# Attention scores of a two-layer hybrid decoder: the keys' high and low parts in one moving operand, the halves summed by VectorE, and attention's stages at later steps

## The chip, the cores and the metric

The kernel runs on one core of a Trainium2 chip. The metric is device time in microseconds (us) of one execution; before the change the median of three runs is 844.93 us (844.09 to 846.22). One more execution was taken with the hardware profiler: it took 844.57 us, of which 842.7 us lie between its first and last instruction. All times inside the kernel are read from that execution.

## The reference

Two decoder layers on 256 tokens of width 2048. The first mixes tokens by forgetting attention (FoX: 32 heads of 64, logits with a decay term), the second by sliding-window attention (SWA: 32 query heads on 4 key heads, window 128, a sink per head, rotary on 16 of 64 dims). Cut to what matters:

```python
# layer 0, per head: causal, 256 keys
s = jnp.einsum('bqhd,bkhd->bhqk', qi.astype(jnp.float32), kf) * scale
s = s + ci[..., None] - c[:, :, None, :]
s = jnp.where(mask[None, None], s, NEG_INF)
p = jax.nn.softmax(s, axis=-1).astype(v.dtype)
return jnp.einsum('bhqk,bkhd->bqhd', p, v)

# layer 1, per head: the block's own 128 keys and the 128 before
m = jnp.maximum(jnp.max(s, axis=-1, keepdims=True), sink)
e = jnp.exp(s - m)
denom = jnp.sum(e, axis=-1, keepdims=True) + jnp.exp(sink - m)
p = (e / denom).astype(v.dtype)

# both layers
p = h @ w_in; ...; y = y * jax.nn.silu(gate); x = x + y @ w_out
```

Everything is float32, with RMSNorm before each layer and at the end.

## The kernel before, in words

**Matrix products in two parts.** Each float32 operand of a projection is split into a high part (a copy in the fp32r format) and a low part (the rest). Activations are split once (`xs`, `ys`: slot 0 high, slot 1 low); each loaded weight tile is split when it arrives: ScalarE casts the high part (L203), VectorE subtracts it (L204), into one of five `w` buffers. A projection is cut into units of 16 input tiles of 128 channels, in parts of four tiles. `block` (around L220) issues, for one part and one half `c` of the unit's columns, four matmuls with a moving operand of 512 columns (high and low side by side: the product of the high stationary part with both) and four with 256 columns (low stationary part, high moving part). The 512-column result has two halves, which the consumers add (`low_half`, L251).

**Order of the work.** TensorE follows the program order of `block` calls over one long stream: FoX input units (q, k, gate, v of eight groups of four heads), the output projection of layer 0, SWA units (k, v, then q and gate of eight groups), the output projection of layer 1. A step counter ticks after every second matmul of a block, so four times per block. Attention is hung on that counter: `after(steps, fn)` runs `fn` so many steps later, with high priority. A group's two pairs of heads (`Pair`, j = 0 and 1) have their score step `s` and transpose steps `t` and `t + 4` in tables: `FOX_DUE = ((16, 34), (40, 60), 106)` means pair 0 scores at 16 and transposes at 34 and 38, pair 1 at 40 and 60, and the values product at 106. `FOX_FIRST` and `FOX_LAST` hold for the first and last FoX group, `SWA_DUE` and `SWA_LAST` for layer 1. For VectorE and ScalarE a scheduler lays the instructions in a fixed order ahead of the run; each engine then takes its own row strictly in that order.

**A pair before the change.** `score` (matmuls at L74) computes, for two heads `hh` and two query blocks (128 queries on 128 keys, 128 queries on 256 keys), query (stationary, its 64 high and 64 low dims stacked) times the keys' high part, then their low part into the same accumulator: eight matmuls, four of 128 and four of 256 columns, in the two buffers of the PSUM pool `ps_s`. `biased` (L293) adds the bias or mask on VectorE and takes the row maximum, in one instruction per head and block. ScalarE exponentiates with row sums (`exps`, L303), VectorE divides (`normalise`: reciprocal L311, four multiplications L314), TensorE transposes the probabilities (`pt`, L77, six transposes of 128x128), ScalarE copies them out (`pts`, L357). `Group.values` multiplies them with v (`psy`), VectorE multiplies by the gate (L389), ScalarE and VectorE write both parts of `ys` (L390, L391).

Of the kernel before, what the change touches and what calls it, by code (L numbers as in the profile page):

```python
# [35 lines left out]
BIAS = 14  # L36
SCALE_DUE = 8


FOX_DUE = ((16, 34), (40, 60), 106)  # L40
FOX_FIRST = ((46, 70), (76, 96), 116)
FOX_LAST = ((14, 32), (38, 72), 86)
SWA_DUE = ((16, 40), (44, 64), 74)
SWA_LAST = ((26, 45), (30, 56), 68)
WBUFS = 5
LOOK = WBUFS - 2
NEG = -1e30
LOWEST = -3.4e38
SCALE = HD ** -0.5
# [3 lines left out]
def trunk(  # L53
# [16 lines left out]
    nc = tc.nc  # L70


    def mm(*args, **kw):
        tc.keep_in_program_order(nc.tensor.matmul(*args, **kw))  # L74
# [26 lines left out]
    def after(steps, fn):  # L101
        due.setdefault(clock[0] + max(steps, 1), []).append(fn)
# [82 lines left out]
    state = {}  # L185
# [23 lines left out]
    def block(unit, p, c):  # L209
# [14 lines left out]

        first, last = kt0 == 0, kt0 + s == KT
        ops = [operands(i) for i in range(s)]
        if unit.halves:

# [55 lines left out]

    BLK = ((slice(0, P), 0), (slice(P, 3 * P), 1))

    def biased(pss, bias, scale):

        st = work.tile([P, 2, 3 * P], F32, tag="st", name="st")
        mx = work.tile([P, 2, 2], F32, tag="mx", name="mx")  # L290
        for hh in range(2):
            for rng, qb in BLK:
                nc.vector.tensor_tensor_reduce(  # L293
                    out=st[:, hh, rng], in0=pss[hh][:, rng], in1=bias(hh, rng), scale=scale,
                    scalar=LOWEST, op0=ALU.add, op1=ALU.max, accum_out=mx[:, qb, hh : hh + 1],
                )
        return st, mx

    def exps(st, nm):
        l = work.tile([P, 2, 2], F32, tag="l", name="l")  # L300
        for hh in range(2):
            for rng, qb in BLK:
                nc.scalar.activation(  # L303
                    st[:, hh, rng], st[:, hh, rng], AF.Exp,
                    bias=nm[:, qb, hh : hh + 1], accum_out=l[:, qb, hh : hh + 1],
                )
        return l

    def normalise(st, l):
        rl = work.tile([P, 2, 2], F32, tag="rl", name="rl")  # L310
        nc.vector.reciprocal(rl, l)  # L311
        for hh in range(2):
            for rng, qb in BLK:
                nc.vector.tensor_scalar_mul(st[:, hh, rng], st[:, hh, rng], rl[:, qb, hh : hh + 1])  # L314

# [8 lines left out]
            nc.vector.tensor_sub(q2[other, hh, :], t[w, :], q2[w, hh, :].bitcast(F32))  # L324
        return q2

    def score(pss, q2, kk):

        for rng, qb in BLK:
            keys = rng.stop - rng.start  # L330
            for hh in range(2):
                q = q2[:, hh, qb * P : (qb + 1) * P]
                for part in range(2):
                    mm(
                        pss[hh][:, rng], q, kk[hh][:, part, 0:keys],
                        start=part == 0, stop=part == 1,
                    )

    class Pair:


        def __init__(self, j, scores, prepare=None):
            self.j, self.scores, self.prepare = j, scores, prepare

        def early(self):
            self.bias = self.prepare()

        def s(self):
            self.st = self.scores()

        def t(self, hh, group):
            pt = ps_t.tile([P, 512], F32, tag="T", name="pt")
# [4 lines left out]
            nc.scalar.copy(group.pts[hh][:, self.j, :], pt[:, 0 : 3 * P])  # L357

        def later(self, group, s, t):
            if self.prepare is not None:  # L360
                after(s - BIAS, self.early)
# [38 lines left out]
    ones_row, z, a = (once[0:H, i * S : (i + 1) * S] for i in range(3))  # L400
# [33 lines left out]
    class FoxGroup(Group):  # L434
# [13 lines left out]
        def k(self, c, ps):  # L448
# [32 lines left out]
        def pair(self, j):  # L481
            h0 = 4 * self.g + 2 * j

            def bias():

                assert "forgot" in state
                bc = fox.tile([P, 2, 3 * P], F32, tag="bc", name="bc")
                nc.gpsimd.dma_start(out=bc, in_=negc_d[h0 : h0 + 2, :].partition_broadcast(P))  # L488
                for hh in range(2):
                    diagonal = bc[:, hh, :].rearrange("p (b k) -> p b k", k=P)[:, 0:3:2, :]  # L490
                    filled = fill_where_not(diagonal, [[0, 2], [-1, P]], 0, 1)
                if h0 == SINK:
# [4 lines left out]
            def scores():  # L497
                pss = [ps_s.tile([P, 512], F32, tag="S", name="ps_s") for _ in range(2)]
                kk = self.kT[j]
                score(pss, self.qT[j], (kk[:, 0], kk[:, 1]))  # L500
                bc = made.bias
                st, mx = biased(pss, lambda hh, rng: bc[:, hh, rng], 1.0)

                c2 = cq[:, :, h0 : h0 + 2]
                nc.vector.tensor_add(mx, mx, c2)  # L505
                nc.vector.tensor_sub(mx, c2, mx)  # L506
                normalise(st, exps(st, mx))
                return st

            made = Pair(j, scores, bias)  # L510
            return made

        def v_of(self, j, b, hh):
            return self.vg[b][:, (2 * j + hh) * HD : (2 * j + hh + 1) * HD]
# [203 lines left out]
    class SwaGroup(Group):  # L718
# [6 lines left out]
        def q(self, c, ps):  # L725
# [3 lines left out]
            if c == 0:  # L729
                self.attend(2 * self.u, SWA_LAST if self.u == 7 else SWA_DUE, self.u == 7, True)  # L730

        def pair(self, j):
            h0 = 4 * self.u + 2 * j
            kv = self.u // 2

            def scores():
                pss = [ps_s.tile([P, 512], F32, tag="S", name="ps_s2") for _ in range(2)]
                kk = state["kk"][:, kv]
                score(pss, self.qT[j], (kk, kk))
                st, mx = biased(pss, lambda hh, rng: smask[:, rng], SCALE)  # L740
# [8 lines left out]
                normalise(st, l)  # L749
                return st  # L750

            return Pair(j, scores)

        def v_of(self, j, b, hh):
            kv = self.u // 2
# [56 lines left out]
    start = [(u, p) for p in range(2) for u in (v0, q0, k0)] + [(v0, 2), (v0, 3), (q0, 2), (k0, 2)]  # L812
# [26 lines left out]
    smask = cpool.tile([P, 3 * P], F32, name="smask")  # L839
# [86 lines left out]
```

## Time and profile before

| what | value |
|---|---|
| median of three runs | 844.93 us |
| profiled execution, its own time | 844.57 us |
| its span, first to last instruction | 842.7 us |
| TensorE (PE) busy | 830.5 us, 99% |
| VectorE (DVE) busy | 656.7 us, 78% |
| ScalarE (ACT) busy | 544.0 us, 65% |
| matmuls | 4970, of them 256 for scores |
| granted TensorE clock | 0.998 |

"Busy" is the share of the span in which an engine executes something. Matmuls overlap, so the time of a stretch of matmuls is best read from the start of the first to the start of what follows. PE is TensorE, PEld its weight loads, DVE VectorE, ACT ScalarE, POOL GpSimd, SP the queue that issues the weight transfers. An entry in square brackets behind a row of the timeline says how long the engine had been idle and what released it.

### The profile page before, as it was taken

Reading aid. Unit: us, or ns where it says so; the run is one execution under the profiler, and the core shown is the slowest. Engines: PE = TensorE matmul, PEld = TensorE weight load, DVE = VectorE, ACT = ScalarE, POOL = GpSimd, SP = SyncE. Lnnn points to the kernel's source line nnn. Section 1 sums busy time; section 2 is a strip of 40 time slices with the busy share of each in tenths; the row PEclk is TensorE's granted clock in tenths of the full one; section 3 lists DMA queues with packets and bytes.
Section 4 is the critical chain, followed back from the end, with each engine's and each line's share of the span. In section 5 each row is a group of like instructions: output and inputs, shape, how many; then the busy total and the mean of one; then the engine's idle time right before and its main releaser. Section 6 shows DMA issues by size and latency. Waiting matters only on the chain.

```text
span 842.7 us, 13482 instructions
## 1 busy us (share of the span) xinstructions
PE 830.5 (99%) x4970; PEld 720.8 (86%) x4970; DVE 656.7 (78%) x1380; ACT 544.0 (65%) x1067; POOL 67.3 (8%) x93
## 2 busy tenths in 40 slices
PE   9999999999999999999999999999999999999996
PEld 7888888888888888888888888888888888888885
DVE  5899868678686877867677778788898889876555
ACT  6678757667475765746655655567766776666552
POOL 1022101001010010100011110000000000003211
PEclk9999999999999999999999999999999999999999
DMA  8666555555464554554465554543444434355522
GB/s 279 239 229 244 188 180 173 190 186 196 157 225 162 171 213 161 187 191 145 162 214 192 200 184 165 180 170 133 167 150 151 157 143 167 133 186 177 194 100 101
DMA packets 26385, 150.51 MB, mean 179 GB/s; under 512 B 3232, under 2 KB 5440, under 8 KB 10704
## 3 DMA queue, kind: packets, MB, share of 16 engines
q1 hardware_dynamic: 23904, 142.22, 48.2%
q0 software_dynamic: 1408, 6.36, 2.2%
q10 hardware_dynamic: 1008, 1.07, 0.4%
q8 instruction: 39, 0.64, 0.3%
q14 instruction: 26, 0.21, 0.1%
HBM read 147.50 MB, written 2.15 MB: 178 GB/s over the span
## 4 chain that ended last, share of the span: by engine, by line
PE 92%; DVE 4%; DMA 1%; ACT 1%; issue 1%; SPq 1%; DVEq 0%; ACTq 0%
PE acc L74 83%; PE ps_s L74 3%; PE psy L74 3%; PE pt L77 2%; DVE w L204 1%; DMA wraw<-in_vf_dram 1%; DMA wraw<-in_fox_in_dram 1%; SPq L198 0%; DVE st L293 0%; ACT st L303 0%; ACT w L203 0%; DVE q L324 0%; DVE xs L155 0%; DVE scaled L669 0%; PE ps_n L74 0%
## 5 line engine op out<-in xcount | busy, mean ns | idle before, releaser
L74 PE MATMUL acc<-xs,w 128*128 128x256 f32 (+1 forms) x2624 | 484.1, 339 | 0.7 <-ACT w L203 0.7
L74 PEld LDWEIGHTS acc<-xs,w 128*128 128x128 f32 x2624 | 405.8, 189 | 61.0 <-issue 3.9
L204 DVE TENSOR_TENSOR w<-wraw,w 128x1024 fp32r<-128x1024 f32 (+4 forms) x275 | 325.7, 1188 | 107.6 <-ACT w L203 105.6
L203 ACT CAST w<-wraw 128x1024 fp32r<-128x1024 f32 (+4 forms) x275 | 278.3, 1016 | 135.6 <-PE acc L74 120.6
L74 PE MATMUL acc<-ys,w 128*128 128x512 f32 x960 | 170.8, 338 | 0.0
L74 PEld LDWEIGHTS acc<-ys,w 128*128 128x128 f32 x960 | 147.4, 189 | 21.5 <-issue 0.6
L74 PE MATMUL acc<-w,xs 128*128 128x256 f32 (+2 forms) x608 | 115.1, 335 | 0.9 <-DVE w L204 0.4
L74 PEld LDWEIGHTS acc<-w,xs 128*128 128x128 f32 x608 | 94.2, 189 | 12.7 <-ACT w L203 1.0
L251 ACT COPY half<-acc 128x256 f32<-128x256 f32 x112 | 41.3, 369 | 58.0 <-PE acc L74 57.3
L303 ACT ACTIVATE st<-st,mx 128x128 f32<-128x128 f32 (+1 forms) x128 | 56.7, 445 | 13.8 <-DVE mx L506 8.4
L575 POOL TENSOR_TENSOR acc<-acc,sq 128x256 f32<-128x256 f32 x28 | 29.8, 1065 | 105.3 <-ACT sq L569 105.3
L357 ACT COPY pts<-pt 128x384 f32<-128x384 f32 x64 | 30.4, 475 | 10.5 <-PE pt L77 10.3
L74 PE MATMUL ps_s<-kk,q 128*128 128x128 f32 (+1 forms) x256 | 35.8, 281 | 0.2
L314 DVE TENSOR_SCALAR st<-st,rl 128x128 f32<-128x128 f32 (+1 forms) x128 | 32.8, 319 | 1.1
L74 PEld LDWEIGHTS ps_s<-kk,q 128*128 128x128 f32 x256 | 32.1, 190 | 1.2 <-issue 0.4
L77 PE MATMUL pt<-ident,st 128*128 128x128 f32 x192 | 31.8, 273 | 1.1 <-DVE st L314 1.1
L573 POOL COPY acc<-sq 128x256 f32<-128x256 f32 x2 | 1.9, 934 | 334.0 <-ACT sq L569 334.0
L121 POOL TENSOR_SCALAR_AFFINE_SELECT bc<-bc 128x256 f32<-128x256 f32 x32 | 22.6, 725 | 51.8 <-DMA bc<-negc_d 51.8
L77 PEld LDWEIGHTS pt<-ident,st 128*128 128x128 f32 x192 | 23.1, 140 | 3.8 <-ACT st L303 1.5
L488 POOL DMA_DIRECT2D bc<-negc_d x16 | 8.8, 552 | 216.3 <-DVE mx L505 139.6
L323 ACT CAST q<-qT 64x256 fp32r<-64x256 f32 x32 | 12.8, 401 | 18.6 <-DVE qT L699 18.2
L155 DVE SCALAR_TENSOR_TENSOR xs<-xT,g_sb,xs 128x256 fp32r<-128x256 f32 x32 | 22.0, 710 | 3.0 <-ACT xs L154 3.0
(133 smaller groups left out, 577.9 us busy)
## 6 DMA issues: line engine op xcount, KB each, us to landing
wraw<-in_fox_in_dram SPq DMA_DIRECT2D x58, 1024.0 KB, 4.9
wraw<-in_swa_in_dram SPq DMA_DIRECT2D x36, 1024.0 KB, 4.8
wraw<-in_fox_out_dram SPq DMA_DIRECT2D x14, 1024.0 KB, 4.9
wraw<-in_swa_out_dram SPq DMA_DIRECT2D x14, 1024.0 KB, 4.9
bc<-negc_d POOLq DMA_DIRECT2D x16, 384.0 KB, 3.9
wraw<-in_fox_in_dram SPq DMA_DIRECT2D x4, 512.0 KB, 5.5
wraw<-in_fox_out_dram SPq DMA_DIRECT2D x4, 512.0 KB, 3.6
wraw<-in_swa_out_dram SPq DMA_DIRECT2D x4, 512.0 KB, 3.5
```

The lines of the kernel that those rows point to most:

```text
L74: tc.keep_in_program_order(nc.tensor.matmul(*args, **kw))
L77: tc.keep_in_program_order(nc.tensor.transpose(out, in_, ident))
L121: return nc.gpsimd.affine_select(out=ap, in_=ap, compare_op=ALU.is_ge, fill=NEG, base=base, pattern=pattern, channel_multiplier=mult,)
L155: nc.vector.scalar_tensor_tensor(out=xs[:, kt, 1, :], in0=xT[:, kt, :], scalar=g, in1=xs[:, kt, 0, :].bitcast(F32), op0=ALU.mult, op1=ALU. ...
L203: state["split"] = nc.scalar.copy(w[:, :, 0, :], raw)
L204: nc.vector.tensor_tensor(out=w[:, :, 1, :], in0=raw, in1=w[:, :, 0, :].bitcast(F32), op=ALU.subtract)
L251: nc.scalar.copy(s, ps[:, S : 2 * S])
L303: nc.scalar.activation(st[:, hh, rng], st[:, hh, rng], AF.Exp, bias=nm[:, qb, hh : hh + 1], accum_out=l[:, qb, hh : hh + 1],)
L314: nc.vector.tensor_scalar_mul(st[:, hh, rng], st[:, hh, rng], rl[:, qb, hh : hh + 1])
L323: nc.scalar.copy(q2[w, hh, :], t[w, :])
L357: nc.scalar.copy(group.pts[hh][:, self.j, :], pt[:, 0 : 3 * P])
L575: nc.gpsimd.tensor_add(sums[0], sums[0], s)
```

## The change

**Scores.** The keys' high and low parts become one moving operand: for the block of 256 keys one matmul per head with 512 columns, for the block of 128 keys one with 256 columns. The two halves of a result are then two products that have to be added. VectorE adds the low half and the bias into `st` (`tensor_add`, L354 and L365 of the changed kernel), and then reduces as before with `st` in the place of the bias (L340). A pair takes three `ps_s` buffers in turn where it took two, and it is done in two steps: the 256-key block at `s`, the 128-key block (`s_first`) `SECOND = 8` steps later, followed by the softmax.

**SWA's division** goes from VectorE to ScalarE: four `nc.scalar.mul` per pair with the reciprocal as a per-row scale (L306).

**Steps.** All five tables move score, transpose and value steps later by 0 to 28 steps.

```diff
-FOX_FIRST = ((46, 70), (76, 96), 116)
-SWA_LAST = ((26, 45), (30, 56), 68)
+FOX_FIRST = ((46, 76), (80, 108), 122)
+SWA_LAST = ((20, 50), (36, 66), 82)
+SECOND = 8
...
-                nc.vector.tensor_tensor_reduce(
-                    out=st[:, hh, rng], in0=pss[hh][:, rng], in1=bias(hh, rng), scale=scale,
-                    scalar=LOWEST, op0=ALU.add, op1=ALU.max, accum_out=mx[:, qb, hh : hh + 1],
-                )
...
+                if scalar:
+                    nc.scalar.mul(p, p, r)
+                else:
+                    nc.vector.tensor_scalar_mul(p, p, r)
...
-                for part in range(2):
-                    mm(
-                        pss[hh][:, rng], q, kk[hh][:, part, 0:keys],
-                        start=part == 0, stop=part == 1,
-                    )
...
+        def product(self, out, hh, qb, keys):
+            q2, kk = self.operands()
+            mm(out, q2[:, hh, qb * P : (qb + 1) * P], kk[hh][:, :, 0:keys], start=True, stop=True)
+        def reduce(self, high, hh, rng, qb):
+            st = self.st[:, hh, rng]
+            nc.vector.tensor_tensor_reduce(
+                out=st, in0=high, in1=st, scale=self.scale, scalar=LOWEST,
+                op0=ALU.add, op1=ALU.max, accum_out=self.mx[:, qb, hh : hh + 1],
+            )
         def s(self):
...
+            for hh in range(2):
+                self.product(pss[hh], hh, qb, S)
+            for hh in range(2):
+                nc.vector.tensor_add(self.st[:, hh, rng], pss[hh][:, S:], self.bias[:, hh, rng])
+                self.reduce(pss[hh][:, 0:S], hh, rng, qb)
+            after(SECOND, self.s_first)
+        def s_first(self):
...
+            for hh in range(2):
+                self.product(ps[:, hh], hh, qb, P)
+            nc.vector.tensor_add(self.st[:, :, rng], ps[:, :, 1, :], self.bias[:, :, rng])
+            for hh in range(2):
+                self.reduce(ps[:, hh, 0, :], hh, rng, qb)
+            self.soft(self.st, self.mx)
```

How the instructions stand, at three places. First TensorE at the first FoX pair's scores (`ps_s`), between blocks of a projection (`acc`); before:

```order
L74 MATMUL acc<-xs,w 128x512 x4
L74 MATMUL acc<-xs,w 128x256 x4
L74 MATMUL ps_s<-kk,q_505 128x128 x4
L74 MATMUL ps_s<-kk,q_505 128x256 x4
L74 MATMUL acc<-xs,w 128x512 x4
```

And in the changed kernel:

```order
L76 MATMUL acc<-xs,w 128x256 x4
L76 MATMUL ps_s<-kk,q_505 128x512 x2
L76 MATMUL acc<-xs,w 128x512 x4
L76 MATMUL acc<-xs,w 128x256 x4
L76 MATMUL acc<-xs,w 128x512 x4
L76 MATMUL acc<-xs,w 128x256 x4
L76 MATMUL ps_s<-kk,q_505 128x256 x2
L76 MATMUL acc<-xs,w 128x512 x4
```

Eight matmuls have become four, and the second two stand two blocks (eight steps) behind the first two.

Second VectorE in the same pair, from its last reduction to the reciprocal (`rl`); `mx` is the row maximum that ScalarE's exponentials wait for, `w` a weight split, `gt` and `gate_e` the gate; before:

```order
L293 ISA st,mx<-ps_s,bc 128x256
L293 ISA mx 128x1
L264 SCALAR_TENSOR_TENSOR gate_e<-gt,gate_e 128x512
L505 TENSOR_TENSOR mx<-mx,cq 128x4
L506 TENSOR_TENSOR mx<-cq,mx 128x4
L204 TENSOR_TENSOR w<-wraw,w 128x4x256
L311 RECIPROCAL rl<-l 128x4
L314 TENSOR_SCALAR st<-st,rl 128x128
```

In the changed kernel, from behind the second addition (`st<-ps_s,bc`, L365) to the reciprocal:

```order
L206 TENSOR_TENSOR w<-wraw,w 128x4x256
L340 ISA st,mx<-ps_s,st 128x128
L340 ISA mx 128x1
L340 ISA st,mx<-ps_s,st 128x128
L340 ISA mx 128x1
L270 TENSOR_TENSOR gt<-gt,gate_e 128x512
L518 TENSOR_TENSOR mx<-mx,cq 128x4
L206 TENSOR_TENSOR w<-wraw,w 128x4x256
L519 TENSOR_TENSOR mx<-cq,mx 128x4
L461 TENSOR_TENSOR q<-acc,half 128x256
L463 TENSOR_TENSOR q<-q,r_494 128x256
L301 RECIPROCAL rl<-l 128x4
```

Two weight splits and a gate multiplication now stand ahead of the second `mx` row, where one gate row stood.

Third TensorE at the last SWA group's values product (`psy`). The part `w_7901` before (`w_7891` after) is the first one that reads the channel tiles 14 and 15 of `ys`, which this product yields; before:

```order
L74 MATMUL psy_7921<-pts_7860,vs_5376 64x512
L74 MATMUL psy_7921<-pts_7860,vs_5376 64x2x128
L74 MATMUL acc_7904<-ys_81,w_7836 128x512 x4
L74 MATMUL acc_7904<-ys_81,w_7836 128x256 x4
L74 MATMUL acc_7945<-ys_81,w_7805 128x512 x4
L74 MATMUL acc_7945<-ys_81,w_7805 128x256 x4
L74 MATMUL acc_7904<-ys_81,w_7870 128x512 x4
L74 MATMUL acc_7904<-ys_81,w_7870 128x256 x4
L74 MATMUL acc_7945<-ys_81,w_7836 128x512 x4
L74 MATMUL acc_7945<-ys_81,w_7836 128x256 x4
L74 MATMUL acc_7808<-ys_81,w_7901 128x512 x4
```

And in the changed kernel:

```order
L76 MATMUL psy_7960<-pts_7875,vs_5376 64x512
L76 MATMUL psy_7960<-pts_7875,vs_5376 64x2x128
L76 MATMUL acc_7934<-ys_81,w_7836 128x256 x4
L76 MATMUL acc_7777<-ys_81,w_7891 128x512 x4
L76 MATMUL acc_7777<-ys_81,w_7891 128x256 x4
```

Four whole blocks stood between the values product and its first reader; now four matmuls of 256 columns do.

More of the change, by code (lines that the diff above doesn't have):

```diff
@@ L37 @@
 SCALE_DUE = 8
-FOX_DUE = ((16, 34), (40, 60), 106)
-FOX_FIRST = ((46, 70), (76, 96), 116)
-FOX_LAST = ((14, 32), (38, 72), 86)
-SWA_DUE = ((16, 40), (44, 64), 74)
-SWA_LAST = ((26, 45), (30, 56), 68)
+FOX_DUE = ((16, 44), (48, 74), 106)
+FOX_FIRST = ((46, 76), (80, 108), 122)
+FOX_LAST = ((14, 40), (44, 72), 88)
+SWA_DUE = ((20, 56), (52, 88), 102)
+SWA_LAST = ((20, 50), (36, 66), 82)
+SECOND = 8
 WBUFS = 5
@@ L285, in trunk @@
     BLK = ((slice(0, P), 0), (slice(P, 3 * P), 1))
[L287 to L293, printed above, removed]
-                    out=st[:, hh, rng], in0=pss[hh][:, rng], in1=bias(hh, rng), scale=scale,
-                    scalar=LOWEST, op0=ALU.add, op1=ALU.max, accum_out=mx[:, qb, hh : hh + 1],
-                )
-        return st, mx
     def exps(st, nm):
@@ L307, in exps, with normalise @@
         return l
-    def normalise(st, l):
+    def normalise(st, l, scalar):
         rl = work.tile([P, 2, 2], F32, tag="rl", name="rl")
@@ L313, in normalise @@
             for rng, qb in BLK:
-                nc.vector.tensor_scalar_mul(st[:, hh, rng], st[:, hh, rng], rl[:, qb, hh : hh + 1])
+                p, r = st[:, hh, rng], rl[:, qb, hh : hh + 1]
+                if scalar:
+                    nc.scalar.mul(p, p, r)
+                else:
+                    nc.vector.tensor_scalar_mul(p, p, r)
     TOP, BOTTOM = slice(0, HD), slice(HD, P)
@@ L325, in stack_q, with __init__ @@
         return q2
[L327 to L332, printed above, removed]
-                for part in range(2):
-                    mm(
-                        pss[hh][:, rng], q, kk[hh][:, part, 0:keys],
-                        start=part == 0, stop=part == 1,
-                    )
     class Pair:
-        def __init__(self, j, scores, prepare=None):
-            self.j, self.scores, self.prepare = j, scores, prepare
+        def __init__(self, j, operands, scale, soft, prepare):
+            self.j, self.operands, self.scale, self.soft = j, operands, scale, soft
+            self.prepare = prepare
@@ L345, in early @@
         def early(self):
             self.bias = self.prepare()
-        def s(self):
-            self.st = self.scores()
+        def product(self, out, hh, qb, keys):
[7 more added lines that the diff above has]
+            )
@@ new lines, in s @@
+        def s(self):
+            self.st = work.tile([P, 2, 3 * P], F32, tag="st", name="st")
+            self.mx = work.tile([P, 2, 2], F32, tag="mx", name="mx")
+            rng, qb = BLK[1]
+            pss = [ps_s.tile([P, 512], F32, tag="S", name="ps_s") for _ in range(2)]
+            for hh in range(2):
[4 more added lines that the diff above has]
+            after(SECOND, self.s_first)
@@ L351, in t @@
+        def s_first(self):
+            rng, qb = BLK[0]
+            ps = ps_s.tile([P, 512], F32, tag="S", name="ps_s")
+            ps = ps.rearrange("p (h a k) -> p h a k", h=2, k=P)
+            for hh in range(2):
[4 more added lines that the diff above has]
+            self.soft(self.st, self.mx)
         def t(self, hh, group):
@@ L359, in later @@
         def later(self, group, s, t):
-            if self.prepare is not None:
-                after(s - BIAS, self.early)
+            after(s - BIAS, self.early)
             after(s, self.s)
@@ L495, in bias, with soft @@
                 return bc
[L497 to L502, printed above, removed]
+            def soft(st, mx):
                 c2 = cq[:, :, h0 : h0 + 2]
@@ L506, in scores, with operands @@
                 nc.vector.tensor_sub(mx, c2, mx)
[L507 to L511, printed above, removed]
+                normalise(st, exps(st, mx), False)
+            def operands():
+                kk = self.kT[j]
+                return self.qT[j], (kk[:, 0], kk[:, 1])
+            return Pair(j, operands, 1.0, soft, bias)
         def v_of(self, j, b, hh):
@@ L734, in pair, with soft @@
             kv = self.u // 2
[L736 to L740, printed above, removed]
+            def soft(st, mx):
                 sk = sink[:, h0 : h0 + 2].unsqueeze(1).to_broadcast([P, 2, 2])
@@ L748, in scores, with operands @@
                 nc.vector.tensor_add(l, l, es)
-                normalise(st, l)
-                return st
-            return Pair(j, scores)
+                normalise(st, l, True)
+            def operands():
+                kk = state["kk"][:, kv]
+                return self.qT[j], (kk, kk)
+            mask = smask.unsqueeze(1).to_broadcast([P, 2, 3 * P])
+            return Pair(j, operands, SCALE, soft, lambda: mask)
         def v_of(self, j, b, hh):
```

## The prediction

> **What bounds the kernel now.** I read the page first: shares of the engines and the chain that ended last.
>
> ```profile
> span 842.7 us, 13482 instructions
> PE 830.5 (99%) x4970; PEld 720.8 (86%) x4970; DVE 656.7 (78%) x1380; ACT 544.0 (65%) x1067; POOL 67.3 (8%) x93
> ...
> PE 92%; DVE 4%; DMA 1%; ACT 1%; issue 1%; SPq 1%; DVEq 0%; ACTq 0%
> ```
>
> TensorE is busy from end to end and carries 92% of the chain. So time is won by giving TensorE less to do, and lost by making it wait. Next, what TensorE waits for, and its two largest waits with a releaser:
>
> ```profile
> PE rows L74 <- DVE tail L656: 2.5, 1, 2.5
> PE warm L74 <- DVE ones L114: 1.1, 1, 1.1
> PE pt L77 <- DVE st L314: 1.1, 1, 1.1
> ```
>
> After the start, attention costs it one visible wait: 1.1 us ahead of one set of transposes (`pt`), released by VectorE's division. Then the price of a matmul, from starts in the timeline and one long piece of the chain:
>
> ```profile
> 741.54 0.63 PE L74 MATMUL acc<-ys,w 128*128 128x512 f32 x2
> 742.01 0.49 PE L77 MATMUL pt<-ident,st 128*128 128x128 f32 x3
> ...
> 416.41 90.01 PE acc L74 x512
> ```
>
> Two 512-column matmuls take 742.01 - 741.54 = 0.47 us, 0.235 us each. The long piece has as many of 512 as of 256 columns and takes 90.01/512 = 0.176 us each, so a pair takes 0.352 and the 256-column one 0.117. A block of four and four: 1.41 us, for four steps. The scores of one pair of heads:
>
> ```profile
> L74 PE MATMUL ps_s<-kk,q 128*128 128x128 f32 (+1 forms) x256 | 35.8, 281 | 0.2
> ...
> 593.29 1.09 PE L74 MATMUL ps_s<-kk,q 128*128 128x128 f32 x8
> 594.22 8.58 PE L74 MATMUL acc<-xs,w 128*128 128x512 f32 x48
> ```
>
> Eight matmuls take 594.22 - 593.29 = 0.93 us. Four of 256 columns are 0.47 of it, so the four of 128 columns take 0.46, 0.115 each: as much as twice the columns.
>
> **The change part by part.** *TensorE.* Per pair, two matmuls of 512 columns (0.47) and two of 256 (0.23) replace the eight: 0.70 in place of 0.93. All of this is on the path. 256/8 = 32 pairs times 0.23 gives **-7.2 us**. Bounds: 0.21 to 0.25 per pair, 6.7 to 8.0.
>
> [...]
>
> *VectorE and ScalarE.* Nearest rows:
>
> ```profile
> L275 DVE TENSOR_TENSOR gt<-acc,half 128x256 f32<-128x256 f32 x32 | 13.4, 420 | 1.8 <-ACT half L251 1.7
> L293 DVE CUSTOM_DVE_ANT_0 st<-ps_s,bc 128x256 f32<-128x256 f32 x32 | 13.4, 419 | 0.0
> L293 DVE CUSTOM_DVE_ANT_0 st<-ps_s,bc 128x128 f32<-128x128 f32 x32 | 9.1, 286 | 1.0 <-PE ps_s L74 1.0
> ...
> 600.39 1.01 DVE L314 TENSOR_SCALAR st<-st,rl 128x128 f32<-128x128 f32 x4
> ...
> L617 ACT ACTIVATE xT<-xT,g_sb 128x256 f32<-128x256 f32 x14 | 7.1, 510 | 0.4
> L653 ACT ACTIVATE diag<-ident,tail 128x128 f32<-128x128 f32 x2 | 0.8, 402 | 0.1
> ```
>
> Three additions that read PSUM, 256 columns each, at 0.42 make 1.26 us of VectorE per pair. The reductions keep their shapes. SWA's division, 1.01 us of VectorE per pair, leaves for ScalarE, 2 x 0.51 + 2 x 0.40 = 1.82. Sums: VectorE +40.3 - 16.2 = +24 us, ScalarE +29 us. Off the path both, so the price is nothing where the stage has room. The stages (first FoX group, a middle FoX group, an SWA group; engines in the order PE, PEld, DVE, ACT, POOL):
>
> ```profile
> 58.00:109.00 51.00, 49.95 (x310) 43.32 (x309) 46.30 (x111) 38.58 (x85) 11.56 (x17) 1.00 0.63 215
> 208.40:258.10 49.70, 49.70 (x302) 43.37 (x301) 37.93 (x77) 31.95 (x62) 3.80 (x6) 1.00 0.53 186
> 589.60:616.80 27.20, 27.20 (x166) 23.19 (x164) 24.30 (x67) 19.16 (x43) 0.00 (x0) 1.00 0.44 153
> ```
>
> Middle FoX group: 37.93 + 2 x 1.26 = 40.5 of 49.2 us; room. SWA group: VectorE 24.30 + 2.52 - 2.02 = 24.8, ScalarE 22.8, of 26.7; little room. The first stage has four pairs in it: 46.30 + 5.0 = 51.3 us, where TensorE would need 51.0 - 4 x 0.23 - 1.05 = 49.0. VectorE is full there, so I expect TensorE to wait there. The first pair's rows show where:
>
> ```profile
> 59.44 1.08 PE L74 MATMUL ps_s<-kk,q 128*128 128x128 f32 x8
> ...
> 64.11 0.28 DVE L293 CUSTOM_DVE_ANT_0 st<-ps_s,bc 128x128 f32<-128x128 f32 x1
> ...
> 65.22 0.68 DVE L264 SCALAR_TENSOR_TENSOR gate_e<-gt,gate_e 128x512 f32<-128x512 f32 x1
> ...
> 66.01 0.16 DVE L506 TENSOR_TENSOR mx<-cq,mx 128x4 f32<-128x4 f32 x1
> 66.09 1.22 DVE L204 TENSOR_TENSOR w<-wraw,w 128x1024 fp32r<-128x1024 f32 x1
> 66.21 0.40 ACT L303 ACTIVATE st<-st,mx 128x128 f32<-128x128 f32 x1 [0.42 <-DVE mx L506]
> ...
> 68.11 0.18 DVE L311 RECIPROCAL rl<-l 128x4 f32<-128x4 f32 x1 [0.80 <-ACT st L303]
> 68.33 1.01 DVE L314 TENSOR_SCALAR st<-st,rl 128x128 f32<-128x128 f32 x4
> 68.78 0.59 PE L77 MATMUL pt<-ident,st 128*128 128x128 f32 x3
> ...
> 81.05 0.61 PE L77 MATMUL pt<-ident,st 128*128 128x128 f32 x3 [1.05 <-DVE st L314]
> ```
>
> VectorE reaches the first pair at 64.11, late, behind older work which the change leaves. In the new order it then does two additions and two reductions (1.68), the gate row (0.68), the third addition (0.42), a split (1.22), two short reductions (0.57), a gate row (0.68), `mx` (0.16), a split (1.22), `mx` (0.16): 6.8 us, up to 70.9. Exponentials up to the reciprocal take 68.11 - 66.21 = 1.90, then 0.22 and the first multiplication 0.29: 73.3. Starts lie closer than durations (1.11 us for four reductions of 1.41), so 72.7 to 73.3. TensorE arrives at the transposes 30 steps after 59.44: seven blocks and a half block of four 512-column matmuls plus the scores, 9.8 + 0.94 + 0.70, at 70.9. It waits about 2.0 us, where it waited for nothing. The second pair waited 1.05 before, with 20 steps behind its whole product; it now has 20 behind the second part of it, two splits in its chain too, but less old work ahead: 0.7 (0 to 1.5) in my estimate. The third gets nothing to 0.8. Together 2.7 for 1.05: **+1.6 us** (bounds -1 to +3.5). The windows' argument, 51.3 - 49.0 = 2.3 us of waiting, lies close to it.
>
> *Layer 1's second pair.* TensorE has, between its second product and its transposes (28 steps), seven blocks and the next group's first product, 7 x 1.41 + 0.47 = 10.3 us. Before:
>
> ```profile
> 605.62 7.16 PE L74 MATMUL acc<-xs,w 128*128 128x512 f32 x40
> ...
> 611.81 1.01 DVE L314 TENSOR_SCALAR st<-st,rl 128x128 f32<-128x128 f32 x4
> 612.61 0.49 PE L77 MATMUL pt<-ident,st 128*128 128x128 f32 x3
> ```
>
> From the end of the scores, 605.62, the first head was divided at about 612.4: 6.8 us. Now an addition and two short reductions replace four (-0.2), ScalarE's two multiplications for that head take 0.9 for 0.6 (+0.3), and two weight splits can stand in the chain (+2.4): 9.3 of 10.3 us. So no wait; the cover is 1 us. The longer cut through a pair also needs `ps_s` back eight steps after the first product, 2.8 us, and two additions and a reduction are 1.3 us: no wait unless VectorE comes 1.5 us late.
>
> *The tail.* The last group's second scores waited for their buffers; and its values product now stands closer to its reader:
>
> ```profile
> 735.53 1.49 PE L74 MATMUL ps_s<-kk,q 128*128 128x128 f32 x8
> 736.86 0.40 PE L74 MATMUL acc<-xs,w 128*128 128x256 f32 x2
> ...
> 752.80 3.54 PE L74 MATMUL acc<-ys,w 128*128 128x512 f32 x18
> ...
> 753.68 0.75 DVE L389 TENSOR_TENSOR gt<-psy,gt 128x256 f32<-128x256 f32 x2
> 754.13 0.74 ACT L390 CAST ys<-gt 128x256 fp32r<-128x256 f32 x2 [1.63 <-DVE gt L389]
> 754.57 0.76 DVE L391 TENSOR_TENSOR ys<-gt,ys 128x256 fp32r<-128x256 f32 x2
> ```
>
> The first wait, 736.86 - 735.53 - 0.93 = 0.40, goes, as the two pairs are now 16 steps apart. After the values product, `ys` for tile 14 is complete at 755.0, 2.2 us later. Before, four blocks covered it, 5.6 us. Now four 256-column matmuls and the two 512-column ones of tiles 12 and 13 do: 0.47 + 0.47 = 0.94. TensorE waits about 1.0 us (0.7, if VectorE is free at once, to 1.3). Net **+0.6**.
>
> **Sum**: -7.2 + 1.6 + 0.6 = -5.0. The profiled execution took 844.57 us, 0.36 below the median of 844.93; from the median this gives **839.9 us**.
>
> **The rivals.** (1) *No new waits*: the scheduler's order leaves VectorE ahead, and both old waits go. 844.93 - 7.2 - 1.05 - 0.4 = 836.3. For it: every table's transposes now stand 18 steps or more behind the second product alone, where before 18 to 34 stood behind the whole; against it, the full first stage. 0.20.
>
> [...] 0.04.
>
> (3) *Slower: VectorE and ScalarE late in each SWA group.* The second pair's chain of 9.3 us grows past 10.3, and TensorE waits once per group, eight times. It decides from one more weight split in the chain: with two (2.4, so 1.4 too late) it costs 11 us, and with 2.1 more (1.1 too late) 8.8, giving 848.7. For it: VectorE is then 93% full (24.8 of 26.7); against it, middle SWA groups show no wait of TensorE now with less cover than 1 us (612.61 follows the division at once). 0.09. (4) *The same at half the size*, 0.4 to 0.9 us per group, or the like in the seven later FoX groups: 843 to 847. 0.15.
>
> **How the numbers follow.** The forecast has 0.52. Two measurements of this kernel can be told apart from about 0.3%, 2.5 us: under 842.4 is faster, over 847.5 slower. Faster: 0.52 + 0.20 = 0.72; same: 0.04 + 0.15 = 0.19; slower: 0.09. The range goes from case (1) into case (4): 836.0 to 844.5. It leaves out (2), (3) and a part of (4).
>
> **What would show it.** Right: 128 score matmuls, a pair's products together at 0.70 us; TensorE's waits for `st` in the first 60 us of attention at 2 to 3 us together and one for `ys` near the end of about 1 us; none in the middle groups. Wrong: waits of TensorE for ScalarE's multiplication (L306) that come back every 27 us, waits ahead of `ps_s`, or a pair's products at 0.9 us.

## The result

The changed kernel takes 849.4 us (median of six runs, 848.74 to 851.88), the kernel before 845.2 us beside it (six runs, 844.09 to 846.22). The ratio is 1.006 with a 95% interval of 1.0049 to 1.0071: slower, by 4.2 us. The forecast was 839.9, faster. The profiled execution took 848.76 us, 4.2 more than that of before.

The page of the changed kernel: shares of the engines, and the chain that ended last by engine.

```profile
span 846.9 us, 13329 instructions
PE 826.4 (98%) x4842; PEld 711.9 (84%) x4842; DVE 669.4 (79%) x1412; ACT 566.7 (67%) x1131; POOL 60.3 (7%) x93
...
PE 86%; DVE 6%; ACT 3%; DMA 2%; SPq 1%; issue 1%; DVEq 0%; ACTq 0%
```

TensorE has 128 matmuls and 4 us of busy time less, but its share of the chain fell from 92% to 86%: other engines now hold it up. What TensorE waited for (in total, times, longest):

```profile
PE ps_s L76 <- DVE q L318: 4.3, 4, 1.1
PE rows L76 <- DVE tail L671: 2.5, 1, 2.5
PE ps_s L76 <- DVE mx L340: 2.3, 1, 2.3
PE acc L76 <- DVE ys L409: 2.3, 1, 2.3
```

Of these only `rows` was there before. The one wait for `pt` has gone. Three things to follow, then, and first the gain. TensorE's timeline of a middle FoX group, from its first scores to those of the next group:

```profile
139.71 0.63 PE L76 MATMUL ps_s<-kk,q 128*128 128x512 f32 x2
140.17 2.96 PE L76 MATMUL acc<-xs,w 128*128 128x512 f32 x16
142.98 0.40 PE L76 MATMUL ps_s<-kk,q 128*128 128x256 f32 x2
143.22 4.36 PE L76 MATMUL acc<-xs,w 128*128 128x512 f32 x24
...
188.98 0.63 PE L76 MATMUL ps_s<-kk,q 128*128 128x512 f32 x2
```

The same two places before:

```profile
137.91 1.09 PE L74 MATMUL ps_s<-kk,q 128*128 128x128 f32 x8
...
187.59 1.09 PE L74 MATMUL ps_s<-kk,q 128*128 128x128 f32 x8
```

A pair's products take 0.46 + 0.24 = 0.70 us, and the group 49.27 in place of 49.68: 0.41 for two pairs, 0.205 each, 6.6 us for 32. The gain is there. The losses:

**First FoX group: 3.1 us.** Rows of TensorE and VectorE that touch the first pair:

```profile
58.91 0.63 PE L76 MATMUL ps_s<-kk,q 128*128 128x512 f32 x2
...
63.41 0.74 DVE L354 TENSOR_TENSOR st<-ps_s,bc 128x256 f32<-128x256 f32 x2
64.07 0.41 DVE L340 CUSTOM_DVE_ANT_0 st<-ps_s,st 128x256 f32<-128x256 f32 x1
...
64.64 0.47 PE L76 MATMUL ps_s<-kk,q 128*128 128x256 f32 x2 [2.32 <-DVE mx L340]
```

VectorE reaches the pair 4.5 us after its product began. The second product stands eight steps behind the first, needs one of the two `ps_s` buffers back, and stood still for 2.3 us. After that the clock was lower for a while (windows of 2 us; the clock is the third number from the end):

```profile
64.00:66.00 2.00, 1.36 (x7) 1.17 (x8) 2.00 (x8) 1.59 (x3) 0.00 (x0) 0.93 0.99 418
66.00:68.00 2.00, 2.00 (x8) 1.81 (x7) 2.00 (x7) 1.03 (x2) 0.55 (x1) 0.50 0.46 120
68.00:70.00 2.00, 2.00 (x10) 1.67 (x10) 1.41 (x4) 0.63 (x3) 0.00 (x0) 0.71 0.95 155
```

From the first scores to the next group's at 139.71 it is 80.80 us, against 137.91 - 59.44 = 78.47 before: 2.3 more, although four pairs had become 0.8 shorter. So the waits and the clock cost 3.1. That is what they add up to: the wait of 2.3, less the 1.05 ahead of `pt` that has gone, and half of the 3.4 us in which the clock was at 0.50 (0.28 + 2.0 + 1.16 in the three windows, if it was at 1.00 in the rest of them; finer windows show 0.50 from 65.75 to 69.00 and 1.00 from 69.25 on), an estimated 1.7, make 3.0.

**SWA groups: 6.0 us.** Rows of VectorE, ScalarE and TensorE around the start of a group:

```profile
616.36 0.42 DVE L714 TENSOR_TENSOR qT<-rot_t,rot 128x256 f32<-128x256 f32 x1
...
616.77 1.05 ACT L205 CAST w<-wraw 128x1024 fp32r<-128x1024 f32 x1
...
617.72 1.50 ACT L306 ACTIVATE st<-st,rl 128x128 f32<-128x128 f32 x4
...
619.12 0.82 ACT L317 CAST q<-qT 64x256 fp32r<-64x256 f32 x2
...
619.79 0.87 DVE L318 TENSOR_TENSOR q<-qT,q 64x256 fp32r<-64x256 f32 x2
...
620.35 0.92 PE L76 MATMUL ps_s<-kk,q 128*128 128x512 f32 x2 [1.08 <-DVE q L318]
```

The rotated query (`qT`) is complete at 616.78; ScalarE casts it only at 619.12, behind a weight cast and the divisions of the second pair of the group before, which has slid this far back. Two groups earlier it was the same, at 565.29 (a row of the same view):

```profile
565.29 0.92 PE L76 MATMUL ps_s<-kk,q 128*128 128x512 f32 x2 [1.08 <-DVE q L318]
```

So two groups take 620.35 - 565.29 = 55.06 us. Before, by the rows of the same pair:

```profile
566.10 1.09 PE L74 MATMUL ps_s<-kk,q 128*128 128x128 f32 x8
...
591.45 0.87 DVE L324 TENSOR_TENSOR q<-qT,q 64x256 fp32r<-64x256 f32 x2 [0.47 <-ACT q L323]
```

One group took 593.29 - 566.10 = 27.19, two 54.38, and they should now take 0.82 less, 53.56. That is 1.5 lost per two groups: the wait of 1.08, and a slower start behind it (the two matmuls take 0.92 in place of the 0.63 of a product that has not waited). Four times 1.5 is 6.0. Why only every second group waits stays open. The query had been complete at 592.32, 0.97 us ahead of its scores.

**Tail: 1.9 us.** The last values product and what reads it:

```profile
759.41 0.75 DVE L407 TENSOR_TENSOR gt<-psy,gt 128x256 f32<-128x256 f32 x2
759.99 1.04 ACT L205 CAST w<-wraw 128x1024 fp32r<-128x1024 f32 x1 [1.76 <-PE acc L76]
760.94 0.71 ACT L408 CAST ys<-gt 128x256 fp32r<-128x256 f32 x2
761.07 1.23 DVE L206 TENSOR_TENSOR w<-wraw,w 128x1024 fp32r<-128x1024 f32 x1 [0.91 <-ACT w L205]
762.21 0.75 DVE L409 TENSOR_TENSOR ys<-gt,ys 128x256 fp32r<-128x256 f32 x2
...
762.68 5.51 PE L76 MATMUL acc<-ys,w 128*128 128x512 f32 x30 [2.27 <-DVE ys L409]
```

Weight work got in between these three dependent steps: the cast, behind one of 1.04, came 0.8 us after its input, and the subtraction behind a split of 1.23. The wait of 2.3 less the 0.40 of before that is gone makes 1.9. The sum, -6.6 + 3.1 + 6.0 + 1.9 = +4.4, against 4.2 measured.

### The profile page after: what moved, and what is told of

Same layout as the page of the kernel before. It is cut to its first block, busy times and chain, and to the rows that moved or that the text cites. A ratio compares the mean times of both kernels' runs of the same rounds, so it can differ in the third digit from the quotient of the medians.

```text
span 846.9 us, 13329 instructions
## 1 busy us (share of the span) xinstructions
PE 826.4 (98%) x4842; PEld 711.9 (84%) x4842; DVE 669.4 (79%) x1412; ACT 566.7 (67%) x1131; POOL 60.3 (7%) x93
## 4 chain that ended last, share of the span: by engine, by line
PE 86%; DVE 6%; ACT 3%; DMA 2%; SPq 1%; issue 1%; DVEq 0%; ACTq 0%
PE acc L76 78%; PE ps_s L76 3%; PE psy L76 3%; PE pt L79 2%; DVE w L206 2%; ACT w L205 1%; SPq L200 1%; DMA wraw<-in_fox_in_dram 1%; ACT st L293 1%; DMA wraw<-in_vf_dram 1%; DVE ssq L804 0%; DVE q L318 0%; DVE xs L157 0%; SPq L792 0%; DVE kk L476 0%
## 5 line engine op out<-in xcount | busy, mean ns | idle before, releaser
L76 PE MATMUL ps_s<-kk,q 128*128 128x256 f32 (+1 forms) x128 | 36.5, 359 | 7.3 <-DVE q L318 4.3
L340 DVE CUSTOM_DVE_ANT_0 st<-ps_s,st 128x128 f32<-128x128 f32 (+1 forms) x128 | 40.2, 352 | 0.2
L76 PEld LDWEIGHTS ps_s<-kk,q 128*128 128x128 f32 x128 | 20.3, 189 | 10.3 <-issue 9.2
L306 ACT ACTIVATE st<-st,rl 128x128 f32<-128x128 f32 x64 | 23.9, 446 | 0.1
L293 ACT ACTIVATION_READ_ACCUMULATOR st<-st,mx 128x1 f32 x128 | 24.0, 187 | 0.0
```

Source lines behind the costliest of these rows:

```text
L293: nc.scalar.activation(st[:, hh, rng], st[:, hh, rng], AF.Exp, bias=nm[:, qb, hh : hh + 1], accum_out=l[:, qb, hh : hh + 1],)
L306: nc.scalar.mul(p, p, r)
L340: nc.vector.tensor_tensor_reduce(out=st, in0=high, in1=st, scale=self.scale, scalar=LOWEST, op0=ALU.add, op1=ALU.max, accum_out=self.mx[:, ...
```

## The experiments

Unless said otherwise each kernel is the changed one with the edit shown. The kernel before, run beside them, took 844.4 to 844.9 us, against 845.2 beside the changed kernel; differences between medians of two series are good to about that much.

**e1: SWA's division back on VectorE.**

```diff
-                normalise(st, l, True)
+                normalise(st, l, False)
```

> The changed kernel with SWA's division back on VectorE, nothing else altered. Theory A (ScalarE's four multiplications stand ahead of the cast of the next group's query, so TensorE waits for that query 1.1 us plus a slow restart, in every second SWA group): the four waits of TensorE for the query (DVE q, 4.3 us in the wait list) go, and the time falls by about 5.8 us, to 843.6 from 849.4. Theory B (VectorE is too full with the additions): VectorE gets 1.0 us more per SWA pair, the four waits stay or grow, and the time is 849 to 853. Theory C (the second SWA pair's softmax was moved by 8 to 16 steps onto the next group's query): the waits stay at about their size, 848 to 851.

847.96 us, ratio 1.0047 (1.0032 to 1.0062). TensorE's wait for the query:

```profile
PE ps_s L76 <- DVE q L318: 0.3, 2, 0.2
```

The other waits stay. Those for the query went from 4.3 to 0.3, the time went little: 1.4 us less, and the intervals of the two ratios overlap. The scores of two SWA groups start at 564.72 and 591.96, 27.24 apart, where 26.8 would be due (27.19 less 0.41). The query now comes just in time, and the slower start, 0.92 for the two matmuls at 564.72, is still there. ScalarE's division is what makes it late in every second group, but not the whole cause.

**e2: without the additions.** This kernel leaves the keys' low parts out of the scores: the low half is multiplied but not added, and the reduction takes the bias as before.

```diff
-                out=st, in0=high, in1=st, scale=self.scale, scalar=LOWEST,
+                out=st, in0=high, in1=self.bias[:, hh, rng], scale=self.scale, scalar=LOWEST,
...
-                nc.vector.tensor_add(self.st[:, hh, rng], pss[hh][:, S:], self.bias[:, hh, rng])
...
-            nc.vector.tensor_add(self.st[:, :, rng], ps[:, :, 1, :], self.bias[:, :, rng])
```

> The changed kernel without the additions of the low halves: the reduction takes the high half and the bias, so the keys' low parts are left out of the scores. VectorE has 96 instructions of 0.42 us less. Theory B: all new waits shrink, those for the query above all; 849.4 - 5.8 for the query, and most of the 2.3 us ahead of the first pair's second product stays as VectorE's lateness there is older work: 841 to 844. Theory A: the waits for the query shrink by at most the 1.3 us that VectorE wins ahead of them, which would hide most of them too, so this run tells A from B only with the run that puts the division back; if the waits stay here, B falls. Theory C: the waits stay; 848 to 850.

846.27 us, ratio 1.0022 (1.0012 to 1.0032).

```profile
PE acc L76 <- DVE ys L407: 2.3, 1, 2.3
PE ps_s L76 <- DVE mx L340: 1.7, 1, 1.7
...
PE ps_s L76 <- DVE q L318: 0.6, 2, 0.4
```

VectorE has 96 additions and 31 us of busy time less (638.8 us), and that takes only 3.1 us off the time. The wait for the buffer is still 1.7 us, that for `ys` unchanged, and `kk` has 2.9 where it had 0.6. So the additions have a part in the waits for `q`, and are not the main cause of the others.

**e3: the kernel before with the new tables of steps alone** (products, reductions and division as before).

```diff
-FOX_DUE = ((16, 34), (40, 60), 106)
+FOX_DUE = ((16, 44), (48, 74), 106)
...
-SWA_DUE = ((16, 40), (44, 64), 74)
+SWA_DUE = ((20, 56), (52, 88), 102)
```

> The kernel before with the later steps alone: its own scores, its division on VectorE, all five step tables of the changed kernel. Theory C: TensorE waits for the query in SWA groups as in the changed kernel, about 1 us in four or more groups, and the last values product costs 2 us as its reader stands 0.94 us behind it: 845.2 + 5.8 + 2.0 = 853. Theories A and B: no waits for the query; only the tail's 2 us, less the 1 us of the first group's old wait: 846 to 847.

858.52 us, ratio 1.0172 (1.0157 to 1.0187).

```profile
PE ps_s L74 <- DVE q L324: 6.4, 7, 1.4
...
PE acc L74 <- DVE ys L391: 2.3, 1, 2.3
```

The steps by themselves cost 14.1 us, with waits for the query in seven groups and the whole wait for `ys`. The two are 8.7 of it. The scores of two middle groups:

```profile
595.01 1.42 PE L74 MATMUL ps_s<-kk,q 128*128 128x128 f32 x8 [0.81 <-DVE q L324]
...
623.53 1.42 PE L74 MATMUL ps_s<-kk,q 128*128 128x128 f32 x8 [0.81 <-DVE q L324]
```

They are 28.52 apart, 1.33 more than before; the wait is 0.81 of it, and the eight matmuls behind it take 1.42 in place of 1.09. Seven times 1.33 is 9.3. Behind the wait for `ys` the granted clock was 0.60 and 0.54 in the two windows from 770 to 774, which is worth another 1.7 by an estimate from these clocks (0.40 and 0.46 of 2 us). With the wait for `ys` itself that makes 13.3 of the 14.1. The wait ahead of the second product (`mx`) is missing here: the product isn't cut.

**e4: SWA's second pair earlier.** Theory: the second pair, begun at step 52, has its softmax where the next query is prepared.

```diff
-SWA_DUE = ((20, 56), (52, 88), 102)
+SWA_DUE = ((20, 56), (40, 76), 102)
```

> The changed kernel with the second SWA pair's scores at step 40 and transposes at 76 in place of 52 and 88, so that its softmax is over before the next group's query comes. Theory C, and A, whose divisions then stand earlier too: the four waits for the query go, 849.4 - 5.8 = 843.6. Theory B (too full as a whole, not at one place): waits move to another place of the group and the time stays within 1.5 us of 849.4.

855.34 us, ratio 1.0135 (1.0118 to 1.0153), and the waits for the query have doubled:

```profile
PE ps_s L76 <- DVE q L318: 8.7, 7, 2.6
```

A miss. As stated the theory falls. As the trace reads, attention's instructions go ahead of weight work, the weight splits pushed back by them are made up afterwards, and they are older than the query's rotation, so they go ahead of it. No run tests this reading by itself.

**e5: the first FoX group's steps later.**

```diff
-FOX_FIRST = ((46, 76), (80, 108), 122)
+FOX_FIRST = ((54, 84), (84, 112), 124)
```

> The changed kernel with the first FoX group's steps 8 and 4 later (FOX_FIRST 54, 84 and 84, 112). Theory: the second product of the first pair waits 2.3 us because VectorE comes to the first additions only at 63.4 us, whatever the step; TensorE then runs 3.4 us at half clock, worth 1.7 us. Eight steps later the buffer is free when TensorE comes: wait and half clock go, 849 - 4.0 = 845. Rival: VectorE is full in this stage, and the wait comes back at the second pair or the next group: 848 to 849.

852.03 us, ratio 1.0089 (1.0075 to 1.0103). The wait for `mx` is 1.8 (2.3 before the edit), that for `kk` 2.1 (0.6). VectorE's additions moved along, from 63.41 to about 66: a later start gives no lead, since both ends of the cut move. The time is 2.6 us longer, which neither outcome of the expectation allowed for.

**e6: the last SWA group's values product earlier.**

```diff
-SWA_LAST = ((20, 50), (36, 66), 82)
+SWA_LAST = ((20, 48), (36, 60), 72)
```

> The changed kernel with the last SWA group's values product at step 72 in place of 82 (transposes 48 and 60). Theory: the 2.3 us that TensorE waits for ys go, as ten steps are 3.5 us: 849 - 2.3 = 846.7. Rival: the transposes, moved 2 and 6 steps ahead, wait for the division instead, or the weights that arrive late there (a cast waited 2.7 us for its transfer) hold TensorE: 848 to 849.

846.79 us, ratio 1.0024 (1.0014 to 1.0033), 2.6 less. The wait for `ys`, 2.3, is gone; the others stay.

**e7: SWA's first pair later**, so that the query has six more steps.

```diff
-SWA_DUE = ((20, 56), (52, 88), 102)
+SWA_DUE = ((26, 62), (52, 88), 102)
```

> The changed kernel with the first SWA pair's scores at step 26 and transposes at 62 in place of 20 and 56. Theory D, formed after the earlier steps made it worse: the query's preparation has no priority, so the second pair's softmax, and the weight splits which that pushes back, stand ahead of it on VectorE and ScalarE; the scores come too early for it by 1.1 to 1.5 us. Six steps are 2.1 us: three of four waits go (the last group keeps its own step), 849 - 4.4 = 844.6. Theory B (engines too full): the wait moves to another place: 848 to 850.

844.66 us, ratio 1.0009 (0.9998 to 1.0019), 4.7 less.

```profile
PE ps_s L76 <- DVE q L318: 0.9, 1, 0.9
```

Only the last group still waits for the query. It has a table of its own, SWA_LAST, in which the change put the first pair's scores at step 20 where they were at 26: earlier, although the section on the change says that all steps move later. A middle group's scores start at 567.30 and 594.05, 26.75 apart: 0.44 less than before the change, the whole gain of two pairs. Six steps more are what the query lacked.

**e8: e5, e6 and e7 together** (FOX_FIRST of e5, SWA_DUE of e7, SWA_LAST ((24, 50), (38, 62), 72), its scores four and two steps later than in e6).

> The changed kernel with all three tables moved: first group 8 and 4 later, first SWA pair 6 later, last group 24, 38 and values at 72. If the three waits are separate: 849 - 4.0 - 5.8 - 2.3 = 837, which is 7 us under the kernel before and leaves the product's own gain. Rival: the order that the scheduler lays out is another one, and new waits take half of it: 841 to 844.

842.85 us, ratio 0.998 (0.9971 to 0.9989): faster than before, but not the 837 of three separate waits. What is left of attention's waits are those of the first stage, `kk` 2.3 and `mx` 1.9.

**e9: e8 with the first FoX group's two pairs in the form of before**, accumulated in one product and without additions, FOX_FIRST ((46, 72), (76, 100), 118).

```diff
+            if self.old:
+                self.s_old()
+                return
...
+            made.old = self.g == 0
```

> The kernel of the three new steps (842.85 us), with the first FoX group's two pairs back in the accumulating form of before, without additions, their steps (46,72) and (76,100). Theory: the additions overfill VectorE in the first stage, so TensorE's waits there (1.9 us for ps_s, 2.3 for kk, and the lower granted clock behind the first, about 1 us more) go for the most part, while two pairs lose 0.21 us each: 842.85 - 3 to 5 + 0.4 = 838 to 840. Rival: VectorE is late there from older work and the new steps, whatever the pairs do: the waits stay at 3 us or more, and the time at 842 to 843.5.

838.22 us, ratio 0.9922 (0.991 to 0.9935). The wait for `mx` is gone, `kk` has 0.7. But this took away two things at once, the additions and the cut.

**e10: e8 with every product as two matmuls.**

```diff
-            mm(out, q2[:, hh, qb * P : (qb + 1) * P], kk[hh][:, :, 0:keys], start=True, stop=True)
...
+            for part in range(2):
+                mm(out[:, part], q2[:, hh, qb * P : (qb + 1) * P], kk[hh][:, part, 0:keys], start=True, stop=True)
```

> The kernel of the three new steps, each product as two matmuls again (keys' high part and low part apart, each into its own half, nothing accumulated; same buffers, additions and steps): 8 matmuls and 1536 columns per pair in place of 4 and 1536. If a matmul of 128 columns costs as much as one of 256 (0.115 against 0.117 us), all of the product's gain is lost, 32 x 0.21 to 0.23: 842.85 + 6.6 to 7.2 = about 849.7 us. [...]

853.62 us, ratio 1.0101 (1.0086 to 1.0117). A middle group's scores:

```profile
192.83 0.64 PE L76 MATMUL ps_s<-kk,q 128*128 128x256 f32 x4
193.31 2.97 PE L76 MATMUL acc<-xs,w 128*128 128x512 f32 x16
196.12 0.56 PE L76 MATMUL ps_s<-kk,q 128*128 128x128 f32 x4
196.52 4.39 PE L76 MATMUL acc<-xs,w 128*128 128x512 f32 x24
...
242.54 0.64 PE L76 MATMUL ps_s<-kk,q 128*128 128x256 f32 x4
```

The group takes 49.71 us, in e8 49.27 as in the changed kernel: 0.22 per pair, 7.0 us in all with the same columns. By the rows the four matmuls of 256 columns take 193.31 - 192.83 = 0.48, where two of 512 took 0.46, and the four of 128 take 196.52 - 196.12 = 0.40, where two of 256 took 0.24. So a matmul of 128 columns took 0.10 us, close to the 0.12 of one of 256, and between these two it was the number of matmuls that set the time; between 256 and 512 columns (0.12 and 0.23) it went with the columns. The other 3.8 us were not expected. Of new waits the trace lists 1.6 for `mx` (in three SWA groups, up to 0.7), 0.9 more than in e8 for weight casts, and 0.8 ahead of a set of transposes; the remainder isn't settled.

**e12: e9 with those two pairs cut in two, eight steps apart, still without additions** (FOX_FIRST of the changed kernel, so its steps are also up to eight later than in e9).

```diff
+            self.half_old(BLK[1], [ps[:, 0:S] for ps in pss])
+            after(SECOND, self.s_last)
```

> The kernel with the first FoX group in the old form (838.22 us), but with those two pairs' products and reductions cut in two eight steps apart, as in the change, still accumulated and without additions, at the changed kernel's steps (46,76), (80,108). Theory cut: the first pair waits because the second part needs a ps_s buffer back while VectorE is still 3.6 us behind with older work; VectorE reaches the pair at 64.1 to 64.7 as ever, two reductions free the buffers at about 65.1, TensorE wants them at 62.5 to 63.3: a wait of 1.5 to 2.5 us for mx, a lower clock behind it, 840 to 842 us. Theory additions: without them VectorE has room, the wait stays under 0.7 us, 838 to 839.5.

842.56 us, ratio 0.9973 (0.9963 to 0.9983). The first pair:

```profile
59.19 0.64 PE L76 MATMUL ps_s<-kk,q 128*128 128x256 f32 x4
63.84 0.41 DVE L382 CUSTOM_DVE_ANT_0 st<-ps_s,bc 128x256 f32<-128x256 f32 x1
...
64.31 0.66 PE L76 MATMUL ps_s<-kk,q 128*128 128x128 f32 x4 [1.68 <-DVE mx L382]
```

With no addition at all the wait is back, and 4.3 us of time with it (`kk` has 2.5 too): the cut is enough for a wait of 1.7. In the changed kernel, with the additions, it was 2.3.

**e11: e8 with the first group's second products 16 steps behind the first**, additions included (FOX_FIRST ((46, 80), (82, 116), 126)).

```diff
-            after(SECOND, self.s_first)
+            after(16 if self.old else SECOND, self.s_first)
...
+            made.old = self.g == 0
```

> The kernel of the three new steps with the first FoX group's pairs in the new form, additions included, but their second products 16 steps behind the first in place of 8, at steps (46,80), (82,116). Theory cut: the buffers are free by then (TensorE comes 2.8 us later than in the changed kernel, which waited 2.3), no wait for mx, and 837.5 to 839.5 us, no worse than with the old form. Theory additions: VectorE stays late, the waits move to kk, q or st, 2 us or more in all, and 840 to 843 us.

838.33 us, ratio 0.993 (0.9917 to 0.9944).

```profile
59.35 0.63 PE L76 MATMUL ps_s<-kk,q 128*128 128x512 f32 x2
63.72 0.75 DVE L354 TENSOR_TENSOR st<-ps_s,bc 128x256 f32<-128x256 f32 x2
...
65.41 0.40 PE L76 MATMUL ps_s<-kk,q 128*128 128x256 f32 x2
```

VectorE comes as late as ever (63.72), with all its additions, and TensorE doesn't wait for it. e11 and e9 are the fastest, 6.4 and 6.7 us below before: about the product's 6.6.

## Why the prediction was wrong

**The product held.** -7.2 was said, 6.6 was measured in the periods, 7.0 from the other side in e10. The chance of 0.04, (2) in the line on the range, was given to a case in which the columns alone set the time of a matmul. No run shows that for 128 columns: e10 has as many columns as e8, so that by them alone its products would have lost nothing, and they lost 7.0; a matmul of 128 columns took 0.10 us there and one of 256 0.12.

**The first group: right cost in the wrong place, and too small.** The step that failed: "two additions and a reduction are 1.3 us: no wait unless VectorE comes 1.5 us late". The prediction had quoted, a few lines above, that VectorE comes to this pair at 64.11 for scores that began at 59.44. The condition was fulfilled, by a row already in hand. The prediction set that lateness against the transposes, 30 steps off, and found 2.0 us; there was no wait there, since TensorE had been held up on the way. The cut was weighed in the part on SWA only, where VectorE is on time. e12 and e11 show it: the wait comes with the cut, 1.7 of it without any addition, and goes with a longer one, additions and all. In place of +1.6 stands +3.1, of which the lower clock behind the wait, 1.7, was not in the sum. That part comes and goes: with the same table for this group, the clock was 0.84, 0.50 and 0.81 in the three windows from 64 to 70 in e7, where the wait was 2.5, and 1.00 in every window from 64 to 74 in e12, where it was 1.7. And the forecast's +1.6 was added up from waits for `pt`, of which there was none.

**SWA: the covered wait was not the only one.** This is the largest error, a term that stood at nothing. The chain of "9.3 of 10.3 us" held: no wait ahead of a transpose in a middle group, and none for L306. But the sum followed the moved pair alone, and never asked what ScalarE and VectorE have to deliver to someone else while it runs. The next group's query had 0.97 us to spare before. The second pair, moved from steps 44 and 64 to 52 and 88, has its exponentials and divisions in front of it now, 1.50 us of these newly on ScalarE (the row of 617.72). That is +6.0 in place of 0. e3 shows that the steps alone do it, e1 that ScalarE's division adds to it, e7 that six steps more for the first pair give back 4.7 of it, all but the last group's. Rival (3) named the second pair's transposes, every group, and 848.7 us: near the measured time by another mechanism. The "wrong if" named L306 and a return every 27 us; it was L318, every 55. The sign beside it, waits ahead of `ps_s`, came true at both places, the first group's `mx` and SWA's query.

**The tail: mechanism right, size wrong.** A wait of about 1.0 for `ys`, up to 1.3; it was 2.3. The price was taken from a place where nothing came between three dependent steps. Here a weight cast and a split did, each of 1.0 to 1.2 us. e6 confirms the place: without the wait 2.6 us less.

Beyond that, VectorE's and ScalarE's loads in an SWA group were forecast well, and misled. (Over the whole run they were put too high: VectorE's busy time rose by 12.7 us where +24 was said, ScalarE's by 22.7 where +29 was.) The window of an SWA group after:

```profile
589.60:616.80 27.20, 27.20 (x160) 22.89 (x159) 23.98 (x65) 22.24 (x55) 0.00 (x0) 1.00 0.47 155
```

VectorE has 24.0 us (24.8 forecast) and ScalarE 22.2 (22.8) of 27: neither is full, and TensorE waited all the same. Room in a stage says nothing of an item's due time.

## What to carry to other kernels

When a product is cut in two, price the return of its buffer at the place where the reader is latest, not where it is on time; the lead needed is the reader's lateness plus what it does first. When stages are moved, list what every engine they touch owes to others in the new place, and how much to spare each of these had before. A gain on the bound engine is safe only once each such margin has been looked up: here four edits to step numbers turned +4.2 us into -6.4.

## What the runs showed of the hardware

**Half the clock after a short wait.** After the TensorE wait of 2.3 us for `mx` in the changed kernel the granted clock was 0.50, for 3.4 us by the windows above. In e7 a wait of 2.5 at the same place was followed by it (0.50 from 66 to 68), in e12 one of 1.7 was not (1.00 from 64 to 74). In e1 the wait for `ys`, also 2.3, was followed by it as well:

```profile
763.00:765.00 2.00, 2.00 (x8) 1.71 (x8) 0.80 (x2) 0.42 (x1) 0.40 (x1) 0.50 0.93 393
```

In the changed kernel's own profile the same wait, of the same length, was followed by 1.00:

```profile
764.00:766.00 2.00, 2.00 (x12) 1.69 (x12) 0.85 (x2) 0.95 (x3) 0.10 (x1) 1.00 0.87 365
```

So waits of 1.7 and 2.3 us were followed by 1.00, and others of 2.3 and 2.5 by 0.50. The length of the wait does not tell the one from the other, and no run shows what does.

**Fewer, wider matmuls.** 128 matmuls saved are worth 6.6 to 7.0 us at the same columns, 52 to 55 ns each on average. By the rows of e10 the gain is nearly all in the 64 saved among those of 128 columns: a matmul of 128 columns took about as long as one of 256 (0.10 and 0.12 us), and one of 512 as long as two of 256 (0.23 and 0.24).
